# A state-space layer whose VectorE operands move to PSUM, and cached attention in four row groups

## The chip, the cores and the metric

The kernel runs on one core of one Trainium2 chip. The metric is the device time of one execution in microseconds; each version was run several times and the median is given. The profile is one further execution, with its own time.

## The reference, cut to what matters

Two layers of a decoder run over a prompt of 512 tokens and over 8 sampled sequences, one new token each. Layer 0 is a state-space mixer (S5) with a gated unit (GLU) and a dense feed-forward (FFN); layer 1 is sparse attention (NSA) and a mixture of 8 experts.

```python
# S5: 64 groups of 16 channels, 64 complex states each
ab = exp(lam * dt)                          # complex decay, from lam_re, lam_im, log_dt
f  = (ab - 1) / lam                         # complex factor
bb = f[..., None] * b                       # input matrices, complex
x  = einsum('blgc,gpc->blgp', rmsnorm(u), bb)
x[:, 0] += ab * h0                          # only the sampled sequences have a state
h  = associative_scan(h_t = ab * h_(t-1) + x_t)          # over 512 tokens
y  = Re einsum('blgp,gcp->blgc', h, c) + d_skip * u
a, b = split(gelu(y) @ w_glu); out = a * sigmoid(b)
# NSA for a sampled sequence: 256 cached rows in 2 pages + window rows + the new row
s = q . k + bias ;  p = softmax(s) ;  o = p . v          # for each branch, then gated
```

## The kernel before, in words

The state-space layer, `s5` (L353 to L702), splits time in 64 blocks of 8 tokens, so that the scan runs over 64 block states and everything inside a block is a matrix product. Its steps:

- Powers `pr`, `pi` of the decay are built by squaring (L451 is the last operation of one), the factors `pfr`, `pfs` at L488 to L490 on VectorE. GpSimd multiplies the gain `gb` into `bb_` ahead of this (L387) and into `dsk` (L492).
- `prod` (L520) makes an outer product of powers with matrices in three operations: two products (L527, L528) and their sum (L529). For each of eight slices `c`, in the order 0, 4, 1, 5, 2, 6, 3, 7, VectorE makes `Pm` with it and GpSimd makes a slice of `Em`. TensorE turns `Pm` (L548), ScalarE copies it to `Wi` (L549), VectorE adds the diagonal to `dsk` (L551) and scales the input by `std` (`U*std`, L555), TensorE multiplies `Wi` with `U` (L559), and ScalarE copies the result to the scan's array `XS` (L562).
- `Tp`, a Toeplitz matrix, is filled by DMAs from `dsk` after slices 5 and 7 (L569).
- `Ar`, `Ai` (L579 to L590) are the ratios of the scan's levels, 32 columns each; short operations of VectorE.
- `step` (L592) is one level of the scan on some columns: two products (L608, L609), their sum (L610), and an addition into `XS` (L611). VectorE does columns 0 to 19, GpSimd 20 to 31 (L614), 6 levels up and 5 down.
- TensorE sums `Tp` x `U` into eight PSUM banks (L662), ScalarE and VectorE copy `XS` to `Hs` (L669), TensorE adds `Em` x `Hs` (L676), ScalarE applies GELU (L679). After a transpose the result goes as a high and a low fp16 half to `GH` (ScalarE, L694) and `GL` (VectorE, L695). Then the GLU begins; its products are L231, its weights are split by ScalarE (L217) and VectorE (L218), and those of the first parts are loaded ahead.

The attention of the sampled sequences is `sample` (L852 to L992), a generator. The prompt's attention is a list of units, and between units one step of `sample` is drawn (L1327); each `yield` in it ends a step. For each of the 8 sequences it loads keys into a buffer `skf` (of 5, `KBUF`, L850) and multiplies them with the queries (L888); sequence b writes 32 rows of one PSUM bank, at 32 x (b // 2), so that neighbours b = 0 and 1 share rows. Later the same is done with the values (L966), with three small fp16 products each (L950).

A scheduler sets the order on each engine from the program's order and its own costs; `PS(...)` (L177) hands out eight PSUM banks in turn, or those named in the call, and a bank that comes round again has to wait for its readers.

Of the kernel before, what the change touches and what calls it, by code (L numbers as in the profile page):

```python
# [9 lines left out]
F32 = mybir.dt.float32  # L10
# [339 lines left out]
def s5(tc, nc, a, o, PS, const, identf, res, wst, prefetch):  # L350
    V, S, G, T = nc.vector, nc.scalar, nc.gpsimd, nc.tensor
    with ExitStack() as es:
# [33 lines left out]
        for b in range(2):  # L386
            G.tensor_tensor(bb_[:, b], bb_[:, b], gb, op=ALU.mult)  # L387
# [73 lines left out]


# [37 lines left out]
        pn = PS()  # L500
# [17 lines left out]
        def prod(eng, d, xr, xi, ks, b1, b2, g, tag):  # L518
            gs = slice(g * GC, (g + 1) * GC)

            def kk(t):
                return t[:, ks, gs].rearrange("p k g -> p g k").unsqueeze(3).to_broadcast([128, GC, 8, 16])

            def bb(t):
                return t[:, gs].unsqueeze(2).to_broadcast([128, GC, 8, 16])
            tmp = tb.tile([128, GC, 8, 16], F32, tag=tag, name=f"{tag}{g}")
            eng.tensor_tensor(d, kk(xr), bb(b1), op=ALU.mult)  # L527
            eng.tensor_tensor(tmp, kk(xi), bb(b2), op=ALU.mult)  # L528
            eng.tensor_tensor(d, d, tmp, op=ALU.add)  # L529
# [8 lines left out]
        for n_, c in enumerate((0, 4, 1, 5, 2, 6, 3, 7)):  # L538
            Pm = wst.tile([128, GC, 8, 16], F32, tag="wh", name=f"Pm{c}")
            prod(V, Pm, pfr, pfs, slice(7, None, -1), b0, b1, c, "tv")  # L540
# [3 lines left out]
            for j0, nj in ((0, 3), (3, 3), (6, 2)):  # L544
                pt = PS()
# [10 lines left out]
            for h in range(2):  # L556
                px = PS()
# [6 lines left out]
            prod(G, Em[:, c * GC:(c + 1) * GC], pr, pi, slice(1, 9), cst, csw, c, "tg")  # L564
# [78 lines left out]
        for half in range(2):  # L643
            py = PS()
# [20 lines left out]
        for _, gs, _ in BLK:  # L665
# [5 lines left out]
            for b in range(gs.start // 4, gs.stop // 4):  # L671
# [119 lines left out]
def nsa(tc, nc, a, o, PS, identf, GH, GL, wload, mm3, act_pool, w1p, HV, hilo, cs):  # L791
# [61 lines left out]
    def sample():  # L853
# [94 lines left out]
        def pvm(rows, p, v, last=False):  # L948
            for i, (x, w) in enumerate(((p[0], v[0]), (p[0], v[1]), (p[1], v[0]))):
# [918 lines left out]
```

## Time and profile before

| | us |
|---|---|
| median of 3 runs | 1564.46 |
| lowest and highest run | 1556.32, 1564.74 |
| the profiled execution | 1557.75 |
| its span in the profile | 1556.0 |
| busy in the span: TensorE, VectorE, ScalarE, GpSimd | 1370.6, 996.6, 773.1, 587.7 |

The mean granted clock of TensorE over the span is 0.945 of full speed. TensorE's 88% is a mean: until about 187 us it is mostly idle, and from there on nearly full. VectorE and GpSimd are the other way round, full in the state-space layer and partly idle behind it. In the rows below an engine's operations carry the line of the kernel, the operation, output <- inputs, and partitions x elements; where several operations form one row, `xN` is their number and the time is that from the first start to the last end.

### The profile page before, as it was taken

What the parts mean: (1) busy time and instruction counts of PE and PEld (TensorE: products, weight loads), DVE (VectorE), ACT (ScalarE), POOL (GpSimd) and SP (SyncE); (2) the same over time, 40 slices, a digit from 0 to 9 for tenths busy, and PEclk for the clock granted to TensorE, in tenths of its full rate; (3) what the DMA queues carried; (4) which work ended last, traced back from release to release, by engine and by line L of the source; (5) the groups of instructions that cost most, each with busy time, mean ns of one, the idle gap of its engine ahead of it and who ended that gap; (6) DMA issues with size and microseconds to landing.
All of it is one profiled execution on the core that took longest, in us unless ns stands there. A gap on an engine that the chain in (4) does not pass through costs nothing.

```text
span 1556.0 us, 37296 instructions
## 1 busy us (share of the span) xinstructions
PE 1370.6 (88%) x15585; PEld 1179.1 (76%) x15585; DVE 996.6 (64%) x1625; ACT 773.1 (50%) x1421; POOL 587.7 (38%) x439
## 2 busy tenths in 40 slices
PE   2173699999999999988989998969998899999895
PEld 1173588988888888865677656854887899999894
DVE  9999456523233223557677759556775688888886
ACT  5051444423233212423687759554755676877663
POOL 5928654222222112221021212322860460743935
PEclk8587899999999999999999999986999999999998
DMA  4023175222322233352401420205989999999885
GB/s 161 0 62 116 57 273 187 79 102 89 109 98 85 85 124 114 132 165 96 157 29 45 147 69 2 84 15 215 364 284 321 351 324 361 378 295 390 320 295 164
DMA packets 82050, 262.36 MB, mean 169 GB/s; under 512 B 25243, under 2 KB 40083, under 8 KB 64339
## 3 DMA queue, kind: packets, MB, share of 16 engines
q1 hardware_dynamic: 78770, 249.24, 46.5%
q0 software_dynamic: 2816, 8.52, 1.6%
q8 instruction: 125, 2.05, 0.5%
q10 hardware_dynamic: 288, 2.14, 0.4%
q14 instruction: 51, 0.41, 0.1%
HBM read 232.30 MB, written 21.67 MB: 163 GB/s over the span
## 4 chain that ended last, share of the span: by engine, by line
PE 60%; DVE 14%; DMA 11%; POOL 5%; ACT 4%; issue 4%; SPq 1%; DVEq 0%; POOLq 0%; ACTq 0%
PE ps L231 29%; PE ps L1686 17%; DMA mf<-in_w_mo 3%; DMA mf<-in_w_mi 2%; PE ps L1034 2%; DMA st<-in_ckc 2%; PE ps L1634 2%; DMA yr<-YS,gidxe 2%; PE ps L1119 1%; DVE ml L1536 1%; PE ps L1245 1%; DVE U L555 1%; DVE st L1235 1%; ACT mh L1535 1%; DVE tl L205 1%
## 5 line engine op out<-in xcount | busy, mean ns | idle before, releaser
L1536 DVE SCALAR_TENSOR_TENSOR ml<-mf,mh 128x2048 f16<-128x2048 f32 (+1 forms) x152 | 312.0, 2055 | 75.6 <-ACT mh L1535 73.3
L1686 PEld LDWEIGHTS <-mh 128*128 128x128 f16 x4224 | 328.6, 98 | 13.5 <-ACT mh L1535 2.4
L1535 ACT ACTIVATE mh<-mf 128x2048 f16<-128x2048 f32 (+1 forms) x152 | 256.1, 1685 | 114.8 <-PE ps L1686 32.3
L1686 PE MATMUL ps<-XE,mh 128*128 128x272 f16 (+7 forms) x2816 | 279.2, 229 | 2.2 <-ACT mh L1535 2.2
L1686 PE MATMUL ps<-XE,ml 128*128 128x272 f16 (+7 forms) x1408 | 261.3, 229 | 4.1 <-DVE ml L1536 4.0
L1766 POOL TENSOR_TENSOR AL<-u,AH 128x272 f16<-128x272 f32 (+3 forms) x88 | 170.9, 1947 | 204.3 <-ACT AH L1765 203.2
L1686 PEld LDWEIGHTS <-ml 128*128 128x128 f16 x2112 | 205.2, 98 | 12.2 <-DVE ml L1536 6.0
L231 PEld LDWEIGHTS <-whf 128*128 128x128 f16 x1408 | 137.7, 98 | 18.5
L231 PE MATMUL ps<-GH,wlf 128*128 128x256 f16 x704 | 137.2, 274 | 0.0
L231 PE MATMUL ps<-GL,whf 128*128 128x256 f16 x704 | 136.8, 274 | 0.0
L231 PE MATMUL ps<-GH,whf 128*128 128x256 f16 x704 | 136.7, 274 | 0.0
L1686 PE MATMUL ps<-AL,mh 128*128 128x272 f16 (+7 forms) x704 | 133.7, 230 | 0.9 <-POOL AL L1766 0.9
L1686 PE MATMUL ps<-AH,ml 128*128 128x144 f16 (+7 forms) x704 | 133.2, 230 | 0.5 <-DVE ml L1536 0.5
L1686 PE MATMUL ps<-AH,mh 128*128 128x144 f16 (+7 forms) x704 | 133.2, 230 | 0.0
L320 POOL TENSOR_TENSOR UL<-sf,UH 128x520 f16<-128x520 f32 x22 | 59.4, 2700 | 175.2 <-ACT UH L319 175.2
L317 DVE SCALAR_TENSOR_TENSOR sf<-ps,sf 128x256 f32<-128x256 f32 (+1 forms) x44 | 17.0, 424 | 140.6 <-PE ps L231 140.6
L217 ACT ACTIVATE whf<-wff 128x2048 f16<-128x2048 f32 x22 | 42.0, 1910 | 95.6 <-issue 77.2
L1235 DVE CUSTOM_DVE_ANT_0 st<-ps,BB 128x512 f32<-128x512 f32 (+3 forms) x128 | 61.4, 484 | 28.9 <-PE ps L1245 26.6
L231 PEld LDWEIGHTS <-wlf 128*128 128x128 f16 x704 | 68.9, 98 | 9.2
L231 PEld LDWEIGHTS <-who 128*128 128x128 f16 x704 | 68.8, 98 | 9.1
L1237 ACT ACTIVATE st<-st,mx 128x512 f32<-128x512 f32 (+3 forms) x128 | 71.6, 561 | 5.9 <-DVE mx L1235 4.6
L203 ACT ACTIVATE th<-ps 128x512 f16<-128x512 f32 (+3 forms) x128 | 54.5, 432 | 35.1 <-PE ps L1245 33.7
(552 smaller groups left out, 3342.6 us busy)
## 6 DMA issues: line engine op xcount, KB each, us to landing
mf<-in_w_mi SPq DMA_DIRECT2D x88, 1024.0 KB, 7.0
mf<-in_w_mo SPq DMA_DIRECT2D x64, 704.0 KB, 5.7
wff<-in_w_fin SPq DMA_DIRECT2D x22, 1024.0 KB, 4.8
wfo<-in_w_fout SPq DMA_DIRECT2D x16, 704.0 KB, 4.0
wfg<-in_w_glu SPq DMA_DIRECT2D x8, 1024.0 KB, 4.9
wfq<-in_w_qk SPq DMA_DIRECT2D x8, 1024.0 KB, 5.0
HS<-z SPq DMA_DIRECT2D x9, 512.0 KB, 8.2
st<-in_ckc SPq DMA_DIRECT2D x16, 256.0 KB, 3.1
```

The source lines that it names most:

```text
L203: S.activation(dh, src, AF.Copy, scale=scale)
L217: S.activation(wh[:, c], wf[:, c], AF.Copy, scale=WS)
L231: T.matmul(t[:, :c1 - c0], w[:, k0 + k, :], x[k][:, c0:c1] if isinstance(x, list) else x[:, k, c0:c1], start=(first and k == 0 and wi == 0 ...
L320: G.tensor_tensor(UL[:, ob, :], sg, UH[:, ob, :], op=ALU.subtract)
L1034: T.matmul(t[:, :n], w[:, k0 + k], x[:, k, c0:c1], start=(k == 0 and i == 0), stop=(k == 7 and i == 2))
L1235: V.tensor_tensor_reduce(out=st[:, :N], in0=pS[:, :N], in1=bias_cur[0][:, r, 512 - N:], scale=1.0, scalar=3.0e38, op0=ALU.add, op1=ALU.min ...
L1237: S.activation(st[:, :N], st[:, :N], AF.Exp, bias=mx, scale=-1.0, accum_out=st8["sums"][:, 1 + br, r:r + 1])
L1535: S.activation(wh, wf, AF.Copy, scale=WS)
L1536: V.scalar_tensor_tensor(wl, wf, WS, wh, op0=ALU.mult, op1=ALU.subtract)
L1634: T.matmul(px[:, :C0 + C7], hts[tb][:n, k * 128:(k + 1) * 128], OHP[:n, tb], start=(tb == 0), stop=(tb == 4))
L1686: T.matmul(ps, w[:, k0 + k, :], x[:, k, :], start=(k == 0 and i == 0), stop=(k == kn - 1 and i == 2))
L1766: al = G.tensor_tensor(AL[r][:, ob], u, AH[r][:, ob], op=ALU.subtract)
```

## The change

- `bb_` and `dsk` times `gb` are done by VectorE, the latter in its old place behind the factors.
- `pfr`, `pfs`, `std`, the second product of `prod` on VectorE, the scan's second product and copies of the ratios (`ArP`, `AiP`, levels 0 to 4) are in PSUM on VectorE's side. An intermediate in PSUM has at most 512 elements, so an operation of 1024 is cut in two and a scan step in pieces of at most 11 rows; two pieces are interleaved.
- Two of the eight `Em` slices (3 and 7) are made by VectorE, from copies of the powers in PSUM.
- VectorE does columns 0 to 21 of the scan, GpSimd 22 to 31.
- The products of TensorE in the slices use banks 5, 6, 7 only. Toeplitz sums 0 to 4 stand ahead of both `Hs` parts, in banks 5, 6, 7, 3, 4; sums 5 to 7 use banks 0, 1, 2, which hold ratios and intermediates of VectorE's scan until it ends. After VectorE's columns come parts 0 to 4, after GpSimd's 5 to 7.
- `sample` loads and multiplies four sequences at a time, all even b, then all odd, so that matmuls that follow each other write different 32-row groups. Ahead of the matmuls of the odd ones stand three more yields.

```diff
-        for b in range(2):
-            G.tensor_tensor(bb_[:, b], bb_[:, b], gb, op=ALU.mult)
...
+        for b in range(2):
+            V.tensor_tensor(bb_[:, b], bb_[:, b], gb, op=ALU.mult)
...
+        pfr, pfs = (PS(b).rearrange("p (k g) -> p k g", k=8) for b in (0, 1))
+        mis = PS(2)
+        tvp = PS(3), PS(4)
...
-        G.tensor_tensor(dsk, dsk, gb, op=ALU.mult)
+        V.tensor_tensor(dsk, dsk, gb, op=ALU.mult)
...
+        std = mis[:, 256:328]
+        V.reciprocal(std, ssum)
...
+        def prod_v(d, xr, xi, ks, o0, b1, b2, g0):
+
+            V.tensor_tensor(d, kk(xr, ks, g0 - o0, GC), bb(b1, g0, GC), op=ALU.mult)
+            tv = [t.rearrange("p (g k c) -> p g k c", g=4, k=8) for t in tvp]
+            for h in range(2):
+                V.tensor_tensor(tv[h], kk(xi, ks, g0 - o0 + 4 * h, 4), bb(b2, g0 + 4 * h, 4), op=ALU.mult)
+            for h in range(2):
+                V.tensor_tensor(d[:, 4 * h:4 * h + 4], d[:, 4 * h:4 * h + 4], tv[h], op=ALU.add)
...
+        EV = (3, 7)
+        ev = [mis[:, 128 * i:128 * i + 128].rearrange("p (k g) -> p k g", k=8) for i in range(2)]
+        for t, x in zip(ev, (pr, pi)):
+            for i, c in enumerate(EV):
+                V.tensor_copy(t[:, :, 8 * i:8 * i + 8], x[:, 1:9, 8 * c:8 * c + 8])
...
+        rat = PS(0)
...
+        V.tensor_copy(ArP, Ar[:, :NL])
+        V.tensor_copy(AiP, Ai[:, :NL])
+        m2p = PS(1), PS(2)
...
+            most = 16 if eng is G else 512 // (2 * w)
+            parts = [(i, min(most, n - i)) for i in range(0, n, most)]
+            while parts:
+                now, parts = parts[:2], parts[2:]
...
+                for m1, m2, tgt in ops:
+                    eng.tensor_tensor(m2, m1, m2, op=ALU.add)
+                for m1, m2, tgt in ops:
+                    eng.tensor_tensor(tgt, tgt, m2, op=ALU.add)
...
-        BLK = ((V, slice(0, 20), "sv"), (G, slice(20, 32), "sg"))
+        BLK = ((V, slice(0, 22), "sv"), (G, slice(22, 32), "sg"))
...
+        def toeplitz(b):
+            py = pys[b] = PS((5, 6, 7, 3, 4, 0, 1, 2)[b])
...
+        for b in range(5):
+            toeplitz(b)
+        for (_, gs, _), bs in zip(BLK, ((0, 1, 2, 3, 4), (5, 6, 7))):
...
-        for b in range(8):
-            f = bp.tile([128, 2, 2, 256], F32, tag="skf", name=f"skf{b}", bufs=KBUF)
...
+        for par in range(2):
+            fs = {}
+            for b in range(par, 8, 2):
+                f = fs[b] = bp.tile([128, 2, 2, 256], F32, tag="skf", name=f"skf{b}", bufs=KBUF)
...
+            for _ in range(3 * par):
+                yield
             for kvp in range(2):
-                T.matmul(ST[rows, :], QS32[:, b % 2, kvp, rows], f[:, kvp].rearrange("p s t -> p (s t)"),
-                         start=(b % 2 == 0 and kvp == 0), stop=(b % 2 == 1 and kvp == 1), skip_group_check=True)
+                for b, f in fs.items():
+                    rows = slice(32 * (b // 2), 32 * (b // 2) + 32)
+                    T.matmul(ST[rows, :], QS32[:, par, kvp, rows], f[:, kvp].rearrange("p s t -> p (s t)"),
+                             start=(par == 0 and kvp == 0), stop=(par == 1 and kvp == 1), skip_group_check=True)
                 yield
```

The values' part of `sample` is changed in the same way, with 1 + 3 x `par` yields ahead of its products.

The change moves instructions at three places that matter here. The first is VectorE's queue around the first products. Names with a number are buffers; `ps_...` is a PSUM bank. Before:

```order
L527 TENSOR_TENSOR Pm_298<-pfr,bb 128x1024
L527 TENSOR_TENSOR Pm_341<-pfr,bb 128x1024
L528 TENSOR_TENSOR tv_299<-pfs,bb 128x1024
L586 TENSOR_TENSOR Ar<-q_668,q_669 128x32
L507 TENSOR_REDUCE ssum<-ps_252 128x72
L529 TENSOR_TENSOR Pm_298<-Pm_298,tv_299 128x1024
```

With the change (lines of the new kernel; L528 is its first product, L531 and L533 are the second and the sum, L606 and L607 the ratios):

```order
L528 TENSOR_TENSOR Pm_304<-ps_236,bb 128x1024
L528 TENSOR_TENSOR Pm_348<-ps_236,bb 128x1024
L531 TENSOR_TENSOR ps_239<-ps_237,bb 128x512
L531 TENSOR_TENSOR ps_240<-ps_237,bb 128x512
L606 TENSOR_TENSOR Ar<-q_684,q_685 128x32
L514 RECIPROCAL ps_238<-ssum 128x72
L533 TENSOR_TENSOR Pm_304<-Pm_304,ps_239 128x512
L533 TENSOR_TENSOR Pm_304<-Pm_304,ps_240 128x512
L607 TENSOR_TENSOR q_684<-Ar,aim 128x32
L546 COPY ps_238<-pr 128x8x8
```

Every product now has a PSUM operand, the second and the sum are two operations each, and the ratio steps between them keep SBUF operands alone.

The second place is ScalarE's queue after the scans. Before:

```order
L669 COPY Hs<-XS 64x1280 x2
L679 ACTIVATE Y<-ps_1011 128x4x8x16
L679 ACTIVATE Y<-ps_1020 128x4x8x16
L679 ACTIVATE Y<-ps_1029 128x4x8x16
L679 ACTIVATE Y<-ps_1038 128x4x8x16
L679 ACTIVATE Y<-ps_1047 128x4x8x16
```

With the change (L708 is the copy of the states, L720 the GELU):

```order
L708 COPY Hs<-XS 64x1408 x2
L720 ACTIVATE Y<-ps_1039 128x4x8x16
L708 COPY Hs<-XS 64x640 x2
L720 ACTIVATE Y<-ps_1048 128x4x8x16
L720 ACTIVATE Y<-ps_1057 128x4x8x16
L720 ACTIVATE Y<-ps_1066 128x4x8x16
```

Before, the copies of GpSimd's columns stood behind five GELU parts and four casts to `GH`; now they stand behind one GELU part.

The third place is TensorE's queue at the keys of the cached sequences (buffer numbers tell the sequences apart). Before:

```order
L888 MATMUL ps_10151<-skf_10152,QS_6930 32x512 x2
L888 MATMUL ps_10151<-skf_10210,QS_6930 32x512 x2
L888 MATMUL ps_10151<-skf_10255,QS_6930 32x512 x2
L888 MATMUL ps_10151<-skf_10315,QS_6930 32x512 x2
L888 MATMUL ps_10151<-skf_10385,QS_6930 32x512 x2
```

With the change:

```order
L935 MATMUL ps_10179<-skf_10180,QS_6958 32x512
L935 MATMUL ps_10179<-skf_10184,QS_6958 32x512
L935 MATMUL ps_10179<-skf_10188,QS_6958 32x512
L935 MATMUL ps_10179<-skf_10192,QS_6958 32x512
L935 MATMUL ps_10179<-skf_10180,QS_6958 32x512
L935 MATMUL ps_10179<-skf_10184,QS_6958 32x512
```

Two matmuls of one sequence followed each other, in one row group; now each matmul is in another row group than the one ahead of it.

## Rows read from the trace of the kernel before

**Rows 1.** Windows: stretch, length, busy us (instructions) by engine, clock, DMA share, GB/s.
```profile
40.00:60.00 20.00, 7.50 (x32) 7.05 (x32) 20.00 (x12) 2.67 (x7) 19.77 (x8) 0.59 0.00 0
140.00:160.00 20.00, 0.00 (x0) 0.00 (x0) 19.28 (x31) 0.00 (x0) 18.51 (x28) 0.50 0.05 15
200.00:250.00 50.00, 50.00 (x454) 44.15 (x453) 27.42 (x27) 18.80 (x28) 22.92 (x13) 1.00 0.76 272
849.00:865.00 16.00, 16.00 (x120) 6.85 (x119) 7.34 (x28) 7.19 (x26) 3.10 (x6) 1.00 0.63 187
909.00:934.00 25.00, 25.00 (x183) 12.57 (x181) 6.89 (x26) 7.71 (x27) 3.00 (x6) 1.00 0.21 64
```
**Rows 2.** The span in 40 slices of 38.9 us, busy tenths of TensorE.
```profile
PE   2173699999999999988989998969998899999895
```
**Rows 3.** Timeline of VectorE, 8 to 92 us: start, us, line, operation.
```profile
10.97 2.42 DVE L427 SCALAR_TENSOR_TENSOR r<-n,r 128x96 f32<-128x96 f32 x1
...
18.58 2.52 DVE L451 TENSOR_TENSOR pr<-t,t 128x192 f32<-128x192 f32 x1
...
24.84 0.68 DVE L488 TENSOR_TENSOR pfr<-pr,fr 128x512 f32<-128x512 f32 x1
25.44 0.69 DVE L488 TENSOR_TENSOR pfs<-pr,fis 128x512 f32<-128x512 f32 x1
...
55.84 19.49 DVE L555 TENSOR_TENSOR U<-U,std 128x576 f32<-128x576 f32 x8
...
80.58 0.31 DVE L551 TENSOR_TENSOR dsk<-ps,dsk 128x48 f32<-128x48 f32 x2
...
88.93 1.21 DVE L527 TENSOR_TENSOR Pm<-pfr,bb 128x1024 f32<-128x1024 f32 x1
90.06 0.29 DVE L551 TENSOR_TENSOR dsk<-ps,dsk 128x48 f32<-128x48 f32 x2
...
91.41 0.18 DVE L587 TENSOR_TENSOR q<-Ar,aim 128x32 f32<-128x32 f32 x1
```
**Rows 4.** Timeline of GpSimd, its products.
```profile
29.25 21.35 POOL L527 TENSOR_TENSOR Em<-pr,cc 128x1024 f32<-128x1024 f32 x8
...
80.57 2.02 POOL L528 TENSOR_TENSOR tg<-pi,cc 128x1024 f32<-128x1024 f32 x1
```
**Rows 5.** Timeline of VectorE, its scan from first to last, and the casts behind.
```profile
113.90 0.83 DVE L609 TENSOR_TENSOR svb<-XS,Ai 128x640 f32<-128x640 f32 x1
...
118.35 2.29 DVE L218 SCALAR_TENSOR_TENSOR wlg<-wfg,whg 128x2048 f16<-128x2048 f32 x1 [0.34 <-ACT whg L217]
...
162.38 0.80 DVE L611 TENSOR_TENSOR XS<-XS,sva 128x600 f32<-128x600 f32 x1
...
174.68 2.49 DVE L695 TENSOR_TENSOR GL<-ps,GH 128x512 f16<-128x512 f32 x4 [8.50 <-ACT GH L694]
```
**Rows 6.** Timeline of GpSimd, the first and last operation of its scan.
```profile
120.04 1.47 POOL L608 TENSOR_TENSOR sga<-XS,Ar 128x384 f32<-128x384 f32 x1 [31.19 <-ACT XS L562]
...
178.38 0.96 POOL L611 TENSOR_TENSOR XS<-XS,sga 128x360 f32<-128x360 f32 x1
```
**Rows 7.** Timeline of TensorE, Toeplitz sums and first four steady GLU matmuls.
```profile
129.76 3.71 PE L662 MATMUL ps<-Tp,U 128*64 128x128 f32 x64
...
186.91 0.62 PE L231 MATMUL ps<-GH,whg 128*128 128x256 f16 x4
```
**Rows 8.** Windows of line L231 alone: the GLU's matmuls before 186.9 us.
```profile
170.00:186.90 16.90, 3.16 (x24) 2.18 (x24) 1.00 0.01 2
```
**Rows 9.** Timeline of TensorE, keys (L888) and values (L966) of cached sequences.
```profile
849.20 5.40 PE L888 MATMUL ps<-skf,QS 128*32 128x512 f32 x20
...
856.53 1.90 PE L888 MATMUL ps<-skf,QS 128*32 128x512 f32 x4
...
909.65 1.91 PE L966 MATMUL ps<-svf,PT 128*32 128x256 f32 x8
```
**Rows 10.** Tile view of the buffers with cached values: microseconds from issue to landing.
```profile
DMA to landing us min/median/max: 2.1/3.5/4.5
```

More of the change, by code (lines that the diff above doesn't have):

```diff
@@ L499, in s5 @@
         ssum = sm.tile([128, 72], F32, name="ssum")
-        pn = PS()
+        pn = PS(5)
         for q in range(8):
@@ L509, in s5, with kk @@
         V.memset(eps, EPS)
-        std = sm.tile([128, 72], F32, name="std")
-        S.activation(std, ssum, AF.Sqrt, bias=eps, scale=1.0 / 1024.0)
-        V.reciprocal(std, std)
+        S.activation(ssum, ssum, AF.Sqrt, bias=eps, scale=1.0 / 1024.0)
+        std = mis[:, 256:328]
+        V.reciprocal(std, ssum)
         Em = p.tile([128, 64, 8, 16], F32, tag="Em", name="Em")
         GC = 8
[L518 to L529, printed above, removed]
+        def kk(t, ks, g0, n):
+            return t[:, ks, g0:g0 + n].rearrange("p k g -> p g k").unsqueeze(3).to_broadcast([128, n, 8, 16])
@@ new lines, in bb @@
+        def bb(t, g0, n):
+            return t[:, g0:g0 + n].unsqueeze(2).to_broadcast([128, n, 8, 16])
+        def prod_v(d, xr, xi, ks, o0, b1, b2, g0):
[5 more added lines that the diff above has]
+                V.tensor_tensor(d[:, 4 * h:4 * h + 4], d[:, 4 * h:4 * h + 4], tv[h], op=ALU.add)
@@ L643, in s5 @@
         for half in range(2):
-            py = PS()
+            py = PS(3 + half)
             for j in range(32):
@@ L670, in s5 @@
                       XS[gh * 64:gh * 64 + 64, 0:64, ri, gs].rearrange("p n g -> p g n"))
-            for b in range(gs.start // 4, gs.stop // 4):
+            for b in bs:
+                if b not in pys:
+                    toeplitz(b)
                 py = pys[b]
@@ L946, in sample, with pvm @@
         nmm = [0]
-        def pvm(rows, p, v, last=False):
-            for i, (x, w) in enumerate(((p[0], v[0]), (p[0], v[1]), (p[1], v[0]))):
-                T.matmul(po[rows, 0:256], x, w, start=(nmm[0] == 0), stop=(last and i == 2), skip_group_check=True)
-                nmm[0] += 1
+        def pvm(rows, p, v):
+            for i, j in ((0, 0), (0, 1), (1, 0)):
+                for r, x, w in zip(rows, p, v):
+                    T.matmul(po[r, 0:256], x[i], w[j], start=(nmm[0] == 0), stop=False, skip_group_check=True)
+                    nmm[0] += 1
@@ new lines, in sample @@
+        for par in range(2):
+            fs = {}
+            for b in range(par, 8, 2):
+                f = fs[b] = bp.tile([128, 2, 2, 256], F32, tag="skf", name=f"svf{b}", bufs=KBUF)
+                for pg in range(2):
+                    page_dma(f[:, 0, pg], a["cvs"], b, pg)
+                nc.sync.dma_start(f[:, 1], a["vwin"][b])
+            rows = [slice(32 * (b // 2), 32 * (b // 2) + 32) for b in fs]
+            pvm(rows, [[t[:15, par, r] for t in (PCH, PCL)] for r in rows],
+                [[t[:, b * 4:b * 4 + 4].rearrange("p k d -> p (k d)") for t in (VSH, VSL)] for b in fs])
+            for _ in range(1 + 3 * par):
+                yield
@@ L965, in sample @@
             for s in range(4):
-                T.matmul(po[rows, 0:256], PT32[:, s, b % 2, rows], f[:, s // 2, s % 2], start=False,
-                         stop=(b % 2 == 1 and s == 3), skip_group_check=True)
-                if s % 2:
-                    yield
+                for r, f in zip(rows, fs.values()):
+                    T.matmul(po[r, 0:256], PT32[:, s, par, r], f[:, s // 2, s % 2], start=False,
+                             stop=(par == 1 and s == 3), skip_group_check=True)
+                yield
```

86 lines of the change are left out of this document (41 added, 45 removed).

## The prediction

> **What bounds the kernel now.** I read the table by windows first: it tells which engine is full in which stretch. From 40 to 60 us VectorE and GpSimd are busy all the time with 12 and 8 operations, while TensorE works 7.50 of 20 us at a granted clock of 0.59; from 140 to 160 us both are nearly full again and TensorE does nothing; from 200 us TensorE is busy 50.00 of 50 us [rows 1]. The slices of the span show it at 9 tenths from there to about 700 us [rows 2]. So the state-space layer is bound by VectorE and GpSimd, and what it gives back becomes a shift of everything behind it.
>
> The timeline of VectorE then says why it is full [rows 3]. Operations of like size have two lengths. A ratio step on 128x32 (L587) takes 0.18 us, but L427 on 128x96 takes 2.42 and a 192-wide L451 2.52; a 512-wide product ends its turn in 0.60 (24.84 to 25.44), yet eight U*std of 576 take 19.49, 2.44 each. GpSimd's 1024-wide products meanwhile take 21.35/8 = 2.67 each, or 2.02 [rows 4]. The long forms have only SBUF operands and last about one GpSimd operation. Forms with an operand in PSUM stay short beside GpSimd: L551, which reads PSUM, needs 0.31 for two at 80.58, inside the GpSimd product that started at 80.57 [rows 3, 4]; four L695, which read PSUM, take 2.49 at 174.68, beside GpSimd's scan [rows 5, 6]. I read this as the two engines taking turns at SBUF, with operations that use PSUM free of it.
>
> Second place: the cached sequences. In 849 to 865 and 909 to 934 TensorE is busy 16.00 and 25.00 us, every moment of them, with VectorE at 7.34 and 6.89 [rows 1]: what TensorE saves there is saved on the path, until VectorE is the next to be late.
>
> **The change, part by part.**
>
> *Products, to the start of VectorE's scan.* From 24.84 to 91.41 are 66.6 us [rows 3]. Undisturbed, the work in it is ten 1024-wide operations at 1.13 (88.93 to 90.06), six 512-wide at 0.60, eight U at 0.60 x 576/512 = 0.67, some 18 short ones near 0.17: 11.3 + 3.6 + 5.4 + 3.0 = 23.3. So 43.3 us are lost to turns. The change leaves about eight operations with SBUF operands alone in this stretch (L490's second products, ratio steps, copies of aim); each can wait for one GpSimd product, 2.0: 16 come back, and the stretch is 39.3.
> Before it, bb*gb and dsk*gb go from GpSimd to VectorE: three 1024-wide, +3.4. In return L427 and the like-sized step before it no longer meet GpSimd (2.4 each instead of some 0.2), nor L451 (2.52 instead of some 0.3): -6.6. Net 3.2 earlier, at 21.6.
> After it, the 22.5 from 91.41 to 113.90 stay. Two Em products come from GpSimd: each 1.13 + 4 x 0.60 = 3.5, so 7.1. The splits of the other products and the copies of powers and ratios into PSUM: 2. VectorE's scan starts at 21.6 + 39.3 + 22.5 + 9.1 = 92.5, 21 earlier than 113.90 [rows 5].
>
> *Scans.* VectorE's columns grow from 20 to 22: 21,120 elements in 67 operations instead of 52. A 640-wide one, 0.83 alone at 113.90, is 0.67 of elements at 0.96 an ns and at most 0.16 fixed, of which some 0.1 show when operations follow each other. 22.0 + 6.7 = 28.7; two L218 casts of 2.29 lie between; 67 results, of which the short ones wait for each other, an estimate of 0.1 more each: 7. In all 40, end 133, where it was 162.38 + 0.80 = 163.2 [rows 5]. GpSimd's scan took 120.04 to 179.34, 59.3 [rows 6]. With 10 columns it has 9,600 elements; at 0.96/360 = 2.7 ns, the rate once VectorE was done, 25.6; small forms cost more than that, an estimate of 0.2 for each of 52, 10; 37 with what still meets VectorE. Its start follows the last copies of XS, 6 behind VectorE's as before, so 100 to 137. In exchange GpSimd hands away two products.
>
> *Tail.* From GpSimd's end (179.34) to steady matmuls of the gated unit at 186.91 are 7.6 us, but 3.16 us of those matmuls had been done in gaps [rows 7, 8]: the equivalent start is 183.8. After, of the eight Toeplitz sums (3.71 in all [rows 7]), three use banks that VectorE's scan holds, so they stand between the scans and the Hs products in TensorE's queue: 1.4, and I add as much again for the waits, since ScalarE's queue now has the second copies of Hs ahead of most Y. 137 + 7.6 + 3.2 + 2.8 = 150.6. **Gain 33; I take 32.** Bounds: 20 if half of the waits that I struck out remain, 40 if next to none of the 16 return. The weight casts and loads queued behind the scan on VectorE and SP move with it.
>
> *The price of PSUM operands.* Rows: 512-wide within SBUF 0.60, L695 from PSUM 2.49/4 = 0.62 [rows 3, 5]. That is 0.02 for each of some 120 operations, 2 us, which the roundings above hold.
> [...]
>
> *Cached sequences.* K: 32 records, two to a matmul; 20 in 5.40, and then three times four in 1.90 [rows 9], 11.1 in all. Four in one row group cost 0.475 each; the first twenty, in which groups change now and then, 0.27: 1.75 times as fast. In the new order eight follow each other in rotation, then single ones between the prompt's units, then the rest. Fourfold, the sum is 6.5; at the 1.75 seen, about 9.3. V: eight records of 256 columns cost 1.91, about 0.23 each without the tail of the last [rows 9]; 64 make 14.9, in rotation 4.9 fourfold, 7.9 at 1.9. The small fp16 products save 0 to 2. So TensorE saves about 9 to 16.
> Against it: a round asks for four buffers out of five, so the second round's transfers wait for the first round's last matmuls. One lands in 3.5 us, at most 4.5 [rows 10]; the three yields ahead of the second round cover that if a unit takes over 1.5. A stall in both parts costs up to 2 x 4.5 and whatever the three transfers add by sharing the queue. **I take 11**, between -3 and 16.
>
> **Sum.** 1557.75 - 32 - 11 = 1515 on the profiled execution, which lies 6.7 below the median of 1564.46 and inside the three runs. The other executions may fall a few us above; I say **1517**. One per cent, 15.6 us, is about what a measurement of this kernel tells from no change: faster means below 1549.
>
> **Rivals.**
> 1. *Half the relief in the state-space layer.* The operations left with SBUF operands meet more than one product each, dependent results in PSUM are later than I put them, GpSimd's scan gets its last XS late. Gain 14 instead of 32: 1535. For: half the levels of the scan are chains of short operations, whose price undisturbed the trace hardly shows. Against: each of the 43 us is read from operations that have a short form in the same timeline [rows 3]. 0.18.
> 2. *Row groups bring nothing*, or the waits for transfers eat it: 1526. For: four of five buffers at once. Against: 0.27 where groups change [rows 9]. 0.13.
> 3. *PSUM frees nothing*, the change doesn't do what it says: the new products write PSUM but may take turns for the SBUF operand that they keep. Then 35 of the 43 stay lost, VectorE's extra 12.4 us and the tail's 2.8 to 5.6 come on top, attention and GpSimd's smaller share give about as much: 1560, no change. Against: L551's second operand is in SBUF too, and it is short [rows 3]. 0.04.
> 4. *Slower.* VectorE takes two cycles for an element where PSUM is one of its operands. Products 24,576 + 6,144 and scan 21,120 elements, 51,800 at 1.04 ns more: +54 - 32 - 11 = 1569. It decides from 0.83 ns more, 1.87 in all. Against: L695, 2.49 for 4 x 512, 1.21 ns with everything in it [rows 5]. 0.03.
>
> **How the numbers follow.** Forecast 0.62, its own range 1500 to 1532. Rival 2 and the greater part of rival 1 lie below 1549, a fifth of rival 1 and rival 3 within 1%, rival 4 with a little of 3 beyond: faster 0.89, same 0.07, slower 0.04. The range begins at 1497, both best bounds (40 and 16, 1502) and 5 for a low execution, and ends at 1542, rival 1 with 2 from the attention.
>
> **What will show it.** U*std near 0.7 us each beside running GpSimd products; VectorE's scan from about 93 to 133, GpSimd's to 137; the gated unit steady near 151, and the work behind it up to the attention about 32 earlier; the first eight K matmuls in 2 to 4 us, and the experts 43 earlier. Wrong would be: long operations with PSUM operands beside GpSimd, a late last XS, TensorE waiting at the Toeplitz sums after both scans, or idle ahead of the second round's matmuls.

## The result and the profile after

The changed kernel takes 1516.64 us (median of four runs, 1514.14 to 1520.94) against 1564.6 before: ratio 0.9703, interval 0.9658 to 0.9748. Run once more as an experiment it came to 0.9704 (0.9682 to 0.9727). The forecast was 1517, in a range of 1497 to 1542.

Its profiled execution is the longest of the four, 1520.94 with a span of 1519.2, so below it is places in the trace that are compared, not ends. First the windows, as in [rows 1]; behind the length stand TensorE's matmuls, its weight loads, VectorE, ScalarE and GpSimd, each with its count, then the granted clock, the DMA share and GB/s:

```profile
40.00:60.00 20.00, 6.46 (x25) 5.98 (x26) 20.00 (x36) 2.32 (x6) 19.29 (x10) 0.50 0.00 0
60.00:80.00 20.00, 18.59 (x98) 17.74 (x98) 16.82 (x37) 8.87 (x24) 6.83 (x8) 0.65 0.00 1
```

VectorE does 36 operations from 40 to 60 us where it did 12, beside a GpSimd that is as busy as before. From 60 to 80 us it is no longer full: TensorE is, with 18.59 of 20 us, at a granted clock of 0.65; cut at 73 us it is 0.50 up to there and 0.97 from there to 90.

VectorE's timeline (start, us, engine, line, operation, and the idle time before it with its releaser where there is one), against [rows 3, 5]:

```profile
21.74 2.39 DVE L451 TENSOR_TENSOR t<-pi,pr 128x384 f32<-128x384 f32 x1
24.06 2.53 DVE L490 TENSOR_TENSOR ps<-pr,fr 128x512 f32<-128x512 f32 x1
...
40.40 1.28 DVE L492 TENSOR_TENSOR ps<-ps,pft 128x512 f32<-128x512 f32 x2
...
58.55 4.73 DVE L572 TENSOR_TENSOR U<-U,ps 128x576 f32<-128x576 f32 x7
...
96.62 0.65 DVE L642 TENSOR_TENSOR sva<-XS,ps 128x484 f32<-128x484 f32 x1
...
117.87 0.94 DVE L642 TENSOR_TENSOR sva<-XS,Ar 128x44 f32<-128x44 f32 x1
118.73 0.97 DVE L643 TENSOR_TENSOR ps<-XS,Ai 128x44 f32<-128x44 f32 x1
119.62 0.19 DVE L642 TENSOR_TENSOR sva<-XS,ps 128x44 f32<-128x44 f32 x1
...
120.22 0.21 DVE L643 TENSOR_TENSOR ps<-XS,ps 128x44 f32<-128x44 f32 x1
...
133.57 0.57 DVE L648 TENSOR_TENSOR XS<-XS,ps 128x396 f32<-128x396 f32 x1
```

Seven U*std take 4.73, 0.68 each, while GpSimd runs; they took 2.44 each. The rows from 117.87 are the mechanism in small. At level 5 the ratios are still in SBUF, and 44 elements cost 0.94 (L642) and 0.97 (L643), about as long as the two GpSimd operations beside them (L642 and L643, 0.93 each). With a ratio in PSUM L643 costs 0.21 at 120.22, wholly inside a GpSimd operation (119.71 to 120.57, shown below). L642's 0.19 at 119.62 says less, since GpSimd is between two operations there. L490 shows the limit: it *writes* PSUM, but both its sources are in SBUF, and it takes 2.53, as L489 with SBUF operands alone did before (2.51 at 27.32); L492, with a source in PSUM, takes 0.64.

GpSimd's timeline (first and last product, then its scan: the first operation, the one beside the row at 120.22, and the last; against [rows 4, 6]):

```profile
21.37 13.89 POOL L537 TENSOR_TENSOR Em<-pr,cc 128x1024 f32<-128x1024 f32 x6 [19.83 <-DVE pr L449]
...
60.76 2.36 POOL L539 TENSOR_TENSOR Em<-Em,tg 128x1024 f32<-128x1024 f32 x1
...
107.68 2.25 POOL L642 TENSOR_TENSOR sga<-XS,Ar 128x320 f32<-128x320 f32 x1 [40.70 <-ACT XS L579]
...
119.71 0.86 POOL L646 TENSOR_TENSOR sgb<-sga,sgb 128x320 f32<-128x320 f32 x1
...
144.68 0.78 POOL L648 TENSOR_TENSOR XS<-XS,sgb 128x300 f32<-128x300 f32 x1
```

It waits 40.70 us for ScalarE's copies of XS, which sets the end of the layer now. ScalarE's queue there, and its tail behind the scans:

```profile
101.42 0.79 ACT L579 COPY XS<-ps 64x288 f32<-64x288 f32 x2 [0.53 <-PE ps L576]
103.67 1.91 ACT L217 ACTIVATE whg<-wfg 128x2048 f16<-128x2048 f32 x1 [1.46 <-DMA wfg<-in_w_glu]
106.80 0.81 ACT L579 COPY XS<-ps 64x288 f32<-64x288 f32 x2 [1.21 <-PE ps L576]
...
134.17 5.24 ACT L708 COPY Hs<-XS 64x1408 f32<-64x1408 f32 x2 [15.68 <-DVE XS L648]
140.59 0.60 ACT L720 ACTIVATE Y<-ps 128x512 f32<-128x512 f32 x1 [1.18 <-PE ps L717]
145.50 2.57 ACT L708 COPY Hs<-XS 64x640 f32<-64x640 f32 x2 [4.31 <-POOL XS L648]
148.09 3.04 ACT L720 ACTIVATE Y<-ps 128x512 f32<-128x512 f32 x6
```

The gated unit begins on TensorE at 155.59 and runs without a gap. TensorE in the cached sequences, against [rows 9]:

```profile
821.50 2.76 PE L935 MATMUL ps<-skf,QS 128*32 128x512 f32 x18
...
828.06 1.02 PE L935 MATMUL ps<-skf,QS 128*32 128x512 f32 x2 [0.91 <-DMA skf<-in_kwin]
...
833.24 1.90 PE L935 MATMUL ps<-skf,QS 128*32 128x512 f32 x10 [0.40 <-DMA skf<-in_kwin]
...
875.41 1.93 PE L1019 MATMUL ps<-svf,PT 128*32 128x256 f32 x32
...
884.72 0.64 PE L1019 MATMUL ps<-svf,PT 128*32 128x256 f32 x8 [1.43 <-DMA svf<-in_cvs]
```

32 records of the values take 1.93, where eight took 1.91. Windows of these lines alone give 6.73 us for the keys (11.11 before) and 6.12 for the values (15.69).

Where the shift is made can be read from first and last starts. Of the prompt's attention units, before and after (line views):

```profile
L1235 DVE CUSTOM_DVE_ANT_0 st<-ps,BB x128: 229/480/693, 766.3 to 980.7; 128x512 f32<-128x512 f32 x32, 128x384 f32<-128x384 f32 x32, 128x256 f32<-128x256 f32 x32, 128x128 f32<-128x128 f32 x32
```

```profile
L1287 DVE CUSTOM_DVE_ANT_0 st<-ps,BB x128: 279/480/693, 738.6 to 941.0; 128x512 f32<-128x512 f32 x32, 128x384 f32<-128x384 f32 x32, 128x256 f32<-128x256 f32 x32, 128x128 f32<-128x128 f32 x32
```

27.7 us earlier at the first, 39.7 at the last: in this execution the state-space layer gave 27.7, the attention 12.0. In another execution of the changed kernel (e9 below) the first unit starts at 733.8 and the last at 936.5: 32.5 and 11.7. The experts' last weight operation is 40.7 earlier in the first of the two (1523.6 to 1482.9); behind it, in the gathering and the last norm, that execution took 3.9 longer (36.3 against 32.4), which no edit touches.

### The profile page after: what moved, and what is told of

Its sections match the earlier page's. It is cut to its first block, busy times and chain, and to the rows that moved or that the text cites. A ratio compares the mean times of both kernels' runs of the same rounds, so it can differ in the third digit from the quotient of the medians.

```text
span 1519.2 us, 37356 instructions
## 1 busy us (share of the span) xinstructions
PE 1363.4 (90%) x15585; PEld 1179.3 (78%) x15585; DVE 968.6 (64%) x1676; ACT 772.2 (51%) x1421; POOL 545.0 (36%) x430
## 4 chain that ended last, share of the span: by engine, by line
PE 55%; DVE 16%; DMA 11%; ACT 5%; issue 5%; POOL 4%; SPq 2%; another core or an unknown queue 0%; DVEq 0%; ACTq 0%; POOLq 0%
PE ps L231 26%; PE ps L1738 16%; DMA mf<-in_w_mo 3%; DMA mf<-in_w_mi 3%; PE ps L1086 3%; DVE ml L1588 2%; PE ps L1686 2%; PE ps L1171 1%; ACT mh L1587 1%; DMA st<-in_ckc 1%; PE ps L1297 1%; DMA yr<-YS,gidxe 1%; PE ps L1284 1%; DVE tl L205 1%; DVE st L1287 1%
## 5 line engine op out<-in xcount | busy, mean ns | idle before, releaser
L1738 PE MATMUL ps<-XE,mh 128*128 128x64 f16 (+7 forms) x2816 | 281.0, 230 | 2.6 <-ACT mh L1587 2.0
L1738 PE MATMUL ps<-XE,ml 128*128 128x96 f16 (+7 forms) x1408 | 262.1, 230 | 3.3 <-DVE ml L1588 3.2
L231 PEld LDWEIGHTS <-whf 128*128 128x128 f16 x1408 | 137.7, 98 | 20.4 <-issue 1.8
L231 PE MATMUL ps<-GH,whf 128*128 128x256 f16 x704 | 135.6, 274 | 0.0
L231 PE MATMUL ps<-GL,whf 128*128 128x256 f16 x704 | 135.6, 274 | 0.0
L231 PE MATMUL ps<-GH,wlf 128*128 128x256 f16 x704 | 135.5, 274 | 0.0
L231 PEld LDWEIGHTS <-who 128*128 128x128 f16 x704 | 68.9, 98 | 9.3
L231 PEld LDWEIGHTS <-wlf 128*128 128x128 f16 x704 | 68.9, 98 | 9.1
L217 ACT ACTIVATE who<-wfo 128x1408 f16<-128x1408 f32 x16 | 22.0, 1377 | 91.6 <-PE ps L231 77.2
```

The costliest lines, as they stand in the source:

```text
L217: S.activation(wh[:, c], wf[:, c], AF.Copy, scale=WS)
L231: T.matmul(t[:, :c1 - c0], w[:, k0 + k, :], x[k][:, c0:c1] if isinstance(x, list) else x[:, k, c0:c1], start=(first and k == 0 and wi == 0 ...
L1738: T.matmul(ps, w[:, k0 + k, :], x[:, k, :], start=(k == 0 and i == 0), stop=(k == kn - 1 and i == 2))
```

## The experiments

The ratios are to the kernel before, run on the same chip.

**The two parts by themselves.** e1 is the changed kernel with the old `sample`, e2 the old kernel with the new one. The core of e1's edit, in the keys (the values go back in the same way):

```diff
-        for par in range(2):
-            fs = {}
-            for b in range(par, 8, 2):
...
-            for _ in range(3 * par):
-                yield
+        for b in range(8):
...
             for kvp in range(2):
-                for b, f in fs.items():
...
+                T.matmul(ST[rows, :], QS32[:, b % 2, kvp, rows], f[:, kvp].rearrange("p s t -> p (s t)"),
```

> The change of the state-space layer alone; the cached sequences are done as before. Theory A (the two gains are apart and add up): in the trace of the changed kernel the attention's first prompt unit came 27.7 us earlier and its last 39.7, so the attention gave 12.0. Without it: 1516.6 + 12 = about 1529, and keys of the cached sequences in 11 us again. Rival B (the attention's gain is only the work in front of it arriving earlier): 1517 to 1520.

> The change of the cached sequences alone; the state-space layer as before. Theory A: 1564.6 - 12 = 1552 to 1553, keys in about 6.6 us of TensorE and values in 6.1. Rival B: the time of before, 1562 or more.

e1: 1530.17 us, ratio 0.9772 (0.973 to 0.9815). e2: 1549.62, 0.9907 (0.9875 to 0.994). 33.9 and 14.4 under 1564.03 add to 48.3; both together gave 48.0 (1564.6 to 1516.64). The gains stand apart, as theory A has it. In e1 the keys' matmuls take 11.11 us again; in e2 keys and values take 6.73 and 6.12.

**What PSUM is worth.**

```diff
-        pfr, pfs = (PS(b).rearrange("p (k g) -> p k g", k=8) for b in (0, 1))
-        mis = PS(2)
-        tvp = PS(3), PS(4)
+        xt = [sm.tile([128, 512], F32, name=f"xt{i}") for i in range(5)]
+        pfr, pfs = (xt[b].rearrange("p (k g) -> p k g", k=8) for b in (0, 1))
+        mis = xt[2]
+        tvp = xt[3], xt[4]
...
-        rat = PS(0)
+        rat = late.tile([128, 512], F32, name="rat")
...
-        m2p = PS(1), PS(2)
+        m2p = late.tile([128, 512], F32, name="m2p0"), late.tile([128, 512], F32, name="m2p1")
```

> The changed kernel with its new share of the work, its splits and its order of steps, but the factors, std, copies of powers, ratios and intermediates of VectorE lie in SBUF tiles of the same shapes instead of PSUM banks. Theory C (VectorE and GpSimd take turns at SBUF, an operand in PSUM frees VectorE): the waits come back, U*std is near 2.4 us each again, some 35 us in the products and 8 to 15 in the scans: 1555 to 1570. Rival D (the gain comes from the new share of the work, and PSUM adds little): 1517 to 1525, U*std near 0.7.

1549.56 us, 0.9899 (0.9861 to 0.9936). That is the time of the attention's part alone (e2): without PSUM operands the new share of work and the new order give the state-space layer nothing. Theory C, the turns at SBUF, holds, and D falls, though less came back than I had put (33 us over the changed kernel, not 38 to 53). The rows of e3 on VectorE say why:

```profile
54.85 5.97 DVE L529 TENSOR_TENSOR Pm<-xt,bb 128x1024 f32<-128x1024 f32 x2
...
68.16 5.43 DVE L573 TENSOR_TENSOR U<-U,xt 128x576 f32<-128x576 f32 x8
...
116.81 0.65 DVE L649 TENSOR_TENSOR XS<-XS,m2p 128x484 f32<-128x484 f32 x1
```

Two products take 5.97, 3.0 each, beside GpSimd. But GpSimd has only 18 products left and is done at 68.2; U*std begins just then and runs free, 0.68 each, where I had looked for 2.4. VectorE's scan starts 14.7 later than in the changed kernel (111.3) and lasts 55.9 instead of 37.5. The scheduler also put VectorE's first Em product ahead of the first Pm here, 6 us that these runs don't part from the rest.

The row at 116.81 prices the operand itself: 484 elements within SBUF, with GpSimd idle (115.10 to 124.36), take 0.65, as the 484 with one source in PSUM do in the changed kernel at 96.62, with GpSimd idle too (66.98 to 107.68). This pair shows no price of a PSUM operand.

e5 and e6 undo one half each: e5 the first four lines of the diff, e6 the last two.

> The changed kernel with the products' part alone back in SBUF (factors, std, copies of powers, second products); the scan keeps its PSUM operands. Without any PSUM operand the kernel took 1549.6, VectorE's scan started 14.7 us later and lasted 18.4 longer. Theory C (turns at SBUF, each part for itself): 1516.6 + 15 to 17 = 1531 to 1534, and the scan again about 37.5 long. Rival (the two parts are not additive, because the later scan no longer overlaps anything): 1540 or more, or under 1525.

> The changed kernel with the scan's part alone back in SBUF (ratios and second products of VectorE's scan); the products keep their PSUM operands. Theory C: VectorE's scan 52 to 56 us instead of 37.5, GpSimd's 45 instead of 37.8; the end of GpSimd's scan decides, +8, and VectorE's, +16 to 18: 1526 to 1534. Rival (GpSimd's end alone decides, VectorE has 11 us of slack): 1522 to 1525.

e6: 1529.09, 0.9803 (0.9773 to 0.9834), some 15 us over the changed kernel; GpSimd's scan ends at 154.5, 9.0 later than in the changed kernel, and VectorE's at 151.9, 17.8 later; the gated unit starts 12.9 later (168.44), so both decide: theory C. VectorE's scan, 60.7 from its first operation, is longer than the 52 to 56 that I had put. e5: 1540.56, 0.9867 (0.9831 to 0.9902): some 24 over the changed kernel (25 by the ratios) rather than 15 to 17, and the rival's 1540. The scan is itself again (GpSimd's 129.5 to 167.2, 37.7), but starts 21 us behind VectorE's: both casts of the gated unit's weights stand in ScalarE's queue ahead of copies of XS, the second with a wait of 1.51 for its DMA at 126.67, and the last copy comes at 128.61. So the halves are not additive (24 and 15, against 33 for both); I read it so that late products move XS into that queue.

**Who makes Em.** e4 gives all eight slices back to GpSimd:

```diff
-        for t, x in zip(ev, (pr, pi)):
-            for i, c in enumerate(EV):
-                V.tensor_copy(t[:, :, 8 * i:8 * i + 8], x[:, 1:9, 8 * c:8 * c + 8])
...
-            if c in EV:
+            if False:
```

> The changed kernel, but GpSimd makes all eight Em slices; VectorE makes none and needs no copies of powers. In the trace of the changed kernel GpSimd is idle from 67 to 107.7 us while VectorE is full, so the two slices on VectorE (7.1 us) are on the path. Theory E: VectorE's scan starts some 5 earlier, 2 being lost again to turns with six more GpSimd products; 1511 to 1514. Rival F (what sets the end is the late start of GpSimd's scan, whose last input came through TensorE's queue): within 1.5 of the changed kernel, 1515 to 1518. Rival G (GpSimd's products were worth moving): 1520 to 1524.

1520.1 us, 0.9719 (0.9674 to 0.9764): no gain, and with the interval no loss that could be told either. The median lies in rival G's range (1520 to 1524) and 2 above F's. Theory E fell on one row of GpSimd's timeline:

```profile
110.12 0.92 POOL L639 TENSOR_TENSOR sga<-XS,Ar 128x320 f32<-128x320 f32 x1 [30.01 <-ACT XS L576]
```

VectorE's scan started 0.8 earlier, not 5, and GpSimd's 2.4 later: ScalarE's last XS, not VectorE, sets that place, as F said. Whether moving the two slices was worth the 2 to 3 us that G would have, these runs don't decide.

**The late XS and the share of the scan.** e7 changes two lines, e8 one:

```diff
-        BLK = ((V, slice(0, 22), "sv"), (G, slice(22, 32), "sg"))
+        BLK = ((V, slice(0, 24), "sv"), (G, slice(24, 32), "sg"))
...
-        for (_, gs, _), bs in zip(BLK, ((0, 1, 2, 3, 4), (5, 6, 7))):
+        for (_, gs, _), bs in zip(BLK, ((0, 1, 2, 3, 4, 5), (6, 7))):
```

```diff
-            py = PS(3 + half)
+            py = PS((2, 2)[half])
```

> The changed kernel with VectorE on 24 columns of the scan and GpSimd on 8, and six of the eight output sums behind VectorE's columns. In the changed kernel VectorE's scan ends at 134.1 and GpSimd's at 145.5, so GpSimd decides. Theory H: two columns are 5 us of GpSimd and 2 of VectorE: ends at 136 and 140, the gated unit 3 to 4 earlier: 1512 to 1514. Rival (the tail behind the scans is bound by ScalarE's copies of the states, which grow for VectorE's part): 1516 to 1518.

> The changed kernel with the sums for the sampled sequences' output (64 pairs of small matmuls, 4.3 us of TensorE) in PSUM bank 2 instead of 3 and 4. That bank is held by VectorE's scan, so that in TensorE's queue they stand behind the last matmuls for XS instead of ahead of them; everything else is the same. In the changed kernel GpSimd's scan starts at 107.7 since the last XS matmul runs only at 105.6, with its input ready at 100.9. Theory I (that queue position is what made GpSimd late): GpSimd's scan starts at 103 to 104 and ends 4 earlier; 1512 to 1514. Rival (ScalarE's cast of the second weights, which waits for a DMA, holds the last copies anyway): start 106 or later, 1516 to 1518.

e7: 1517.85, 0.9738 (0.9707 to 0.977). e8: 1521.41, 0.975 (0.9716 to 0.9783). Neither is better. In e7 GpSimd's scan is indeed shorter (33.2 instead of 37.8), but from its end to the gated unit 14.3 us pass instead of 10.1, and the unit starts at 151.21, 1.1 before that of e9. ScalarE in e7, then TensorE's transposes behind it:

```profile
131.18 7.94 ACT L708 COPY Hs<-XS 64x1536 f32<-64x1536 f32 x4 [16.33 <-DVE XS L648]
143.50 4.03 ACT L720 ACTIVATE Y<-ps 128x512 f32<-128x512 f32 x8 [4.39 <-PE ps L699]
...
146.60 4.67 PE L729 MATMUL ps<-identf,Y 64*128 64x64 f32 x56 [0.27 <-ACT Y L720]
```

All copies come first, and all eight GELUs wait for TensorE's sums: the rival's tail. Some 2 of the 4 us go with TensorE's clock: the 64 transposes take 5.4 us here, at a granted clock of 0.57 in the stretch of the row shown (56 in 4.67, 0.083 each), and 3.26 in the changed kernel, at 0.91 (0.051 each). In e8 the sums moved as meant, but ScalarE then held the last XS, as that rival said:

```profile
99.94 0.80 ACT L579 COPY XS<-ps 64x288 f32<-64x288 f32 x2 [1.13 <-PE ps L576]
101.86 1.91 ACT L217 ACTIVATE whg<-wfg 128x2048 f16<-128x2048 f32 x1 [1.13 <-DMA wfg<-in_w_glu]
103.80 0.81 ACT L579 COPY XS<-ps 64x288 f32<-64x288 f32 x2
...
150.42 4.03 ACT L720 ACTIVATE Y<-ps 128x512 f32<-128x512 f32 x8 [4.79 <-PE ps L699]
```

From the copy before to the last one 3.9 us pass, instead of 5.4 (101.42 to 106.80). GpSimd's scan starts at 104.69, between theory I's 103 to 104 and the rival's 106, but VectorE's starts earlier as well (93.23, for a reason given at the clock below): GpSimd is 11.5 behind it, and 11.1 and 12.3 in the two executions of the changed kernel. Nothing was gained at that place. The displaced pairs (L685, L686) now run on TensorE between 129.4 and 141.6, behind VectorE's scan; the long run of `Hs` products begins at 141.75 instead of 139.47, and all eight GELUs wait as in e7. From GpSimd's end to the gated unit it is 17.1 instead of 10.1, again with the transposes at a low clock (0.51, 56 of them in 5.09).

**TensorE's clock.** e9 is the changed kernel unedited; e10 adds the first piece, e11 both:

```diff
+        pw = PS(6)
+        for i in range(14):
+            T.matmul(pw, identf, idc[0][:, 0:4, 0:128], start=True, stop=True)
         for n_, c in enumerate((0, 4, 1, 5, 2, 6, 3, 7)):
...
+            if n_ == 0:
+                pw = PS(5)
+                for i in range(3):
+                    T.matmul(pw, identf, idc[0][:, 0:4, 0:128], start=True, stop=True)
```

> The changed kernel once more, without any edit, so that the two kernels sent with it have it on their own chip. About 0.970 of the kernel before.

> The changed kernel with 14 extra matmuls of 512 columns, whose results nobody reads, between the norm's sums and the first product matmul, to keep TensorE busy from about 26 us on. In the changed kernel TensorE is idle from 25.7 to 48.4, runs the slices' matmuls at a granted clock of 0.50 from 57.7 and is full from there to 72; it is granted 1.00 only from about 73. Theory J (the lower clock is the next bound of the state-space layer): if the clock stays up from the extra work to the slices, the last XS comes 4 to 7 us earlier, and the time is 0.966 to 0.968 of before. Rival K (TensorE pauses from 52.5 to 57.7, and the clock is low again behind it): no gain, 0.969 to 0.971. Rival L (the extra work ends later than 48 and holds the first product up): 0.972 or more.

> As the one before, with three more such matmuls behind the first slice's, in the pause from 52.5 to 57.7. Theory J: the clock is up through the slices, the windows from 56 to 72 show 1.00 instead of 0.50, the last XS 4 to 7 us earlier: 0.966 to 0.968. Rival (VectorE is as full there as TensorE, so that a faster TensorE only waits): 1 to 2 us, 0.969.

e9: 1516.97, 0.9704. e10: 1520.65, 0.9717 (0.9693 to 0.9742). e11: 1515.03, 0.9693 (0.9667 to 0.972). All the same. The windows of e11 show that the edit missed its aim:

```profile
26.00:38.00 12.00, 12.00 (x28) 5.07 (x28) 12.00 (x7) 2.41 (x3) 11.92 (x7) 1.00 0.00 0
38.00:48.00 10.00, 0.12 (x1) 0.00 (x0) 10.00 (x13) 0.35 (x1) 9.69 (x5) 0.76 0.00 0
48.00:56.00 8.00, 4.18 (x16) 3.86 (x16) 8.00 (x16) 1.53 (x4) 7.76 (x4) 0.50 0.00 0
56.00:64.00 8.00, 0.63 (x1) 0.50 (x2) 8.00 (x15) 0.00 (x0) 7.69 (x6) 0.50 0.00 0
64.00:72.00 8.00, 7.30 (x35) 4.74 (x34) 6.82 (x24) 2.06 (x5) 3.00 (x5) 0.81 0.01 2
```

The 14 matmuls ran at 1.00 and were over by 38 us; ten idle us later the clock was 0.50 again. The edits also changed the order on VectorE: in both, TensorE's next matmul behind the first slice waits until 63.4 for an addition to `dsk` that now stands behind U*std (57.7 in the changed kernel), in e11 with the three others first. So theory J, that the half clock sets the start of the scans, is not decided by these two. What bears on it are other executions of the same stretch. The changed kernel's profile, then that of e9:

```profile
56.00:72.00 16.00, 13.93 (x59) 13.42 (x60) 14.16 (x30) 5.15 (x13) 10.67 (x10) 0.50 0.00 1
```

```profile
56.00:72.00 16.00, 12.32 (x83) 11.53 (x83) 16.00 (x32) 7.16 (x19) 10.92 (x10) 0.89 0.00 1
```

With 0.89 instead of 0.50 TensorE gets 83 matmuls done instead of 59 from 56 to 72, VectorE is full instead of waiting 1.8 us, its scan starts at 91.96 instead of 96.62, and the gated unit at 152.30 instead of 155.59. But 1.8 of these 4.7 us were there before: in e9 one step of VectorE missed a turn of GpSimd. The changed kernel, then e9:

```profile
33.25 2.56 DVE L491 TENSOR_TENSOR pft<-pi,fi 128x512 f32<-128x512 f32 x1
```

```profile
33.31 0.68 DVE L491 TENSOR_TENSOR pft<-pi,fi 128x512 f32<-128x512 f32 x1
```

The cleaner pair is e8, whose edit touches nothing that runs before 97 us. VectorE's rows in it lie within 0.07 us of the changed kernel's up to 69.7, and from 60 to 65 TensorE does 24 matmuls in each. From 65 to 72, the changed kernel and then e8:

```profile
65.00:72.00 7.00, 6.65 (x30) 6.30 (x29) 5.16 (x16) 2.70 (x8) 1.98 (x3) 0.50 0.01 2
```

```profile
65.00:72.00 7.00, 5.42 (x43) 4.84 (x41) 7.00 (x19) 4.55 (x13) 2.03 (x4) 1.00 0.01 2
```

At 1.00 instead of 0.50 TensorE is in time, VectorE has none of the changed kernel's waits (1.84 us ahead of 71.70, 1.02 ahead of 73.54), and its scan starts at 93.23 instead of 96.62. So 0.50 instead of 1.00 in this stretch costs 3.4 us at the start of VectorE's scan. What that is worth in the kernel's time no run shows, since e8's tail is its own; between the changed kernel and e9 the gated unit differs by 3.3 with both causes in it.

**The order inside a round.** e12 keeps loads and rounds but gives each sequence its matmuls in a row:

```diff
-            for kvp in range(2):
-                for b, f in fs.items():
+            for b, f in fs.items():
+                for kvp in range(2):
...
-                yield
+                if b // 2 % 2:
+                    yield
...
-            for s in range(4):
-                for r, f in zip(rows, fs.values()):
+            for r, f in zip(rows, fs.values()):
+                for s in range(4):
```

> The changed kernel with the same loads, the same four buffers at a time and the same number of yields in the cached sequences' attention, but the matmuls of one sequence follow each other (two for the keys, four for the values), so that the row group changes only from sequence to sequence. Theory M (rotation over row groups is what saves TensorE's time): keys near 11 us again and values near 15 instead of 6.6 and 6.1, less what the fp16 products keep, 1.8: 1517 + 9 to 12 = 1526 to 1529, about 0.977. Rival N (fewer and larger rounds are what helps, the order inside a round does not): 0.970 to 0.972.

1528.12 us, 0.9792 (0.9769 to 0.9814): 11.2 over e9 (1516.97), and 13.7 by the ratios (0.9792 against 0.9704), so the attention's gain of 14.4 is nearly all gone, as theory M has it. TensorE in e12:

```profile
818.73 3.62 PE L935 MATMUL ps<-skf,QS 128*32 128x512 f32 x20
...
873.22 4.59 PE L1020 MATMUL ps<-svf,PT 128*32 128x256 f32 x32
```

32 records of values take 4.59 with four matmuls to a group in a row, 1.93 in rotation. All values take 13.19, all keys 9.31.

## Why the prediction was right

- **Turns at SBUF.** The reading of [rows 3, 4] is confirmed by e3, e5 and e6 (33, 24 and 15 us over the changed kernel) and by the rows from 117.87 to 120.22. I had let L490 go free in the sum as one of the operations that use PSUM; its PSUM is only the target, and it cost 2.53 and 2.52. The stretch also began at 24.06 where I had 21.6: GpSimd's first product starts at 21.37, and a step of the powers that ran free before now meets it (L451, 2.39 for 384 elements; its L453 of before took 0.55).
- **VectorE's scan** ran from 96.6 to 134.1; forecast 92.5 to 133. The start is 4 late and the length 37.5 instead of 40, with 68 operations and not 67: the estimates of what an operation costs beyond its elements were too high. 484-wide ones start 0.57 apart at 97.18 and 88-wide ones 0.16 at 116.86: 1.04 ns an element, as the forecast has it (0.96 an ns), and 0.07 beyond the elements. In e9 the start is 91.96, on the forecast. Between the two lie the turn at 33 us (1.8) and TensorE between 56 and 72 us, at 0.50 and at 0.89: with VectorE's waits gone it is the next that can be late. I had not asked that of TensorE, though [rows 1] show it at 0.59.
- **GpSimd's scan** took 37.8, forecast 37, but started at 107.7, not 100. "6 behind VectorE's as before" is the step that failed. The 6 was counted from L609 at 113.90 [rows 5], but that is not the first operation of the scan. The kernel before, then the changed one:

```profile
109.13 0.82 DVE L608 TENSOR_TENSOR sva<-XS,Ar 128x640 f32<-128x640 f32 x1
...
111.22 1.22 DVE L529 TENSOR_TENSOR Pm<-Pm,tv 128x1024 f32<-128x1024 f32 x1
```

```profile
94.32 0.68 DVE L533 TENSOR_TENSOR Pm<-Pm,ps 128x512 f32<-128x512 f32 x1
```

From first operation to first operation GpSimd was 10.9 behind VectorE before and is 11.1 now, 12.3 in e9. What did grow is the way from VectorE's last `Pm` to GpSimd's start: 7.6 before (112.44 to 120.04), 12.7 now. On it the copies of the last XS stand behind two casts in ScalarE's queue, one with a wait of 1.46 for its DMA, and the pairs of sums stand in TensorE's queue. In e8, without the pairs, it is 13.1; no run moved the casts, so what each of them costs is not shown. The late start cost less than 7.7, since `Hs` copies, sums and GELU for VectorE's columns run in that time.

- **Tail.** 10.1 from GpSimd's end to the gated unit, without matmuls done ahead; I had 7.6 + 3.2 + 2.8 = 13.6. The start is 155.6 instead of 150.6 in this execution, 152.3 in e9; the gain 27.7 and 32.5, and 33.9 between medians in e1, where I had 32. So GpSimd's scan ended 8.5 late, and the shorter tail gave 3.5 of that back; in e9 it is 5.1 and 3.4.
- **Attention.** 12.0 and 11.7 in the two executions, 14.4 between medians in e2; forecast 11. Matmuls of keys and values gave 14, more than the factor of 1.75 on which I set the lower end: about fourfold in the values' first round (32 records in 1.93, eight in 1.91 before). The second rounds' loads cost 1.3 and 1.4 us in TensorE's waits, which I had only in the bounds.
- **The rivals.** PSUM operands that free nothing are refuted by U*std, 0.68 instead of 2.44 beside GpSimd's products, and PSUM operands that add 1.04 ns an element by 0.65 for 484 elements, with a source in PSUM as within SBUF. "Half the relief" (14) is refuted by 27.7 and more, "row groups bring nothing" by e2 (14.4) and e12.
- **The sum.** 48.0 between medians, of which 43 were forecast against the profiled execution and 47 against the median of 1564.46. Between medians both parts gave a little more than I took. The mechanism held, but that the median came within 0.4 us of 1517 is luck: scans that start 4 and 8 late, a tail 3.5 shorter, a better attention and the 2 us allowed between executions cancelled, and the runs of the changed kernel alone lie up to 6.8 apart.

## What to carry to other kernels

When two engines have their operands in SBUF, look for operations of one form with two lengths (before the change L489, 0.69 at 26.71 and 2.51 at 27.32), and compare forms by where their *sources* are: here one source in PSUM freed VectorE (U*std, 2.44 to 0.68), a target in PSUM alone did not (L490, 2.53). Small matmuls that use a quarter of the output rows are worth ordering in rotation over the quarters, one by one and not in runs: 32 records of the values took 1.93 so, and 4.59 in runs of four (e12). And when a wait is taken away, ask of every engine behind it, whether it is in time for the earlier start; here the queues of ScalarE and TensorE, not VectorE, set the new end (GpSimd's scan waits until 107.68 for ScalarE's copies of XS).

## What the runs showed that I had not expected

- Beside a GpSimd product VectorE with a PSUM target and two SBUF sources took 2.53 for 512 elements (L490), 0.64 with one source in PSUM (L492).
- The clock granted to TensorE in the same stretch of the same code was 0.50 in one execution and 0.89 in another (56 to 72 us). Where the clock alone differed (1.00 in e8, 0.50 in the changed kernel, 65 to 72 us) VectorE's scan began 3.4 us earlier with the higher one. In e11 it was 1.00 in a stretch of twelve busy us and 0.50 after ten nearly idle ones.
- Moving two Em slices between VectorE and GpSimd (e4), or two columns of the scan (e7), is no longer worth anything that can be measured; in the traces GpSimd's start and the tail wait for TensorE and ScalarE.
